# Attention of a prefix-GQA trunk layer: exponentials left in PSUM for 38 of 64 latent heads, turned before they are normalised, and a new order of the stage

## The chip, the core and the metric

The kernel runs on one core of one Trainium2 chip. The metric is the device time of one execution in microseconds. TensorE is PE, VectorE is DVE, ScalarE is ACT, GpSimd is POOL, SyncE is SP; PEld is TensorE's loading of the stationary operand, and SPq is SP's sequencer, which issues the DMAs.

## What is computed

One trunk layer for 128 context tokens and 512 latent tokens, in float32 (the products are made of a rounded high part and a low part, three matmuls for one). What the change touches is the attention of the mixer; 16 query heads share 4 key and value heads of 64 columns.

```python
def one_block(qblk):
    s = jnp.einsum('bqkgd,btkd->bkgqt', qblk, k).astype(jnp.float32) * scale
    p = jax.nn.softmax(s, axis=-1).astype(v.dtype)
    return jnp.einsum('bkgqt,btkd->bqkgd', p, v)
...
    u = rms_norm(h, p["g_pre1"]) * (1 + sc1) + sh1
    mo, k, v = mixer(u, p, rope_tabs, ctx_k, ctx_v)     # q, k normed and rotated, then block_attention, then w_att_out
    h = h + g1 * rms_norm(mo, p["g_post1"])
    u = rms_norm(h, p["g_pre2"]) * (1 + sc2) + sh2
    h = h + g2 * rms_norm(conv_ffn(u, p), p["g_post2"])
```

Context tokens attend to the 128 context keys, latent tokens to 128 cached keys and 512 latent keys, 640 in all.

## The kernel before

**Stages.** A first stage (0 to about 66 us) makes the modulated tokens `UH`, `UL` (high and low part) and the products for keys and values. The attention stage (66 to 268 us) is what the change is about. Behind it come the output projections, the convolution mixer and the feed-forward layer, which are long runs of matmuls against weights that stream in.

**The attention stage is a list of pieces and a plan.** The code makes `works`: each `Work` has a name, an engine (sometimes two or three to choose from), the works it comes after, and `Room`s, places in memory that it shares with other works. The string `PLAN` then gives the order in which the pieces are written out: a number of a work, a letter for the engine chosen, and digits for the places taken (`follow`, L705). On PE, ACT, DVE, POOL and SP the instructions stay in this order; each engine runs its own in order, and waits where its next one is not ready. So a piece that is late holds up whatever stands behind it on its engine.

**One step.** 36 steps: four groups of heads, each with one step for the context tokens (steps 0, 9, 18 and 27, four heads of 128x128 at once) and eight for latent tokens (128 query rows, two heads, written n.0 and n.1). A latent step goes so:

- `s` (L1107, PE): scores of both heads, 12 matmuls into two areas of PSUM, 640 columns each. There are three areas of two banks each (`AREAS`); two more banks, 6 and 7, hold query tiles, gate products and outputs.
- `max` (L1152, DVE): the negated row maximum, read from PSUM.
- `exp` (L1155, ACT): the exponential, from PSUM into one of four tiles `E` of SBUF; its row sum is accumulated. With it the area of PSUM is free.
- `part` (L1075, POOL or DVE) and `inv` (L1077, DVE): the sum times 2 to the power -15, and its reciprocal, one pair for each head.
- `share` (L1167, POOL), for the 25 heads that `POOL_WAY` marks: E times the reciprocal.
- `P1` (L1170, ACT): the high half of the probabilities as float16, for the other 39 heads with the reciprocal as a scale.
- `P2` (L1175 POOL for the 25, L1177 DVE for the 39): the low half, E (times the reciprocal) minus P1. P1 and P2 lie in one of four tiles `P`.
- `T` (L1185, SP): a DMA that transposes the tile `P` into one of five tiles `PT`.
- `pv` (L1204, PE): 30 matmuls of `PT` with the values, into bank 6 or 7. After two steps the output is complete: `AH` (L1214, ACT) writes its high part, scaled by the values' factor, `AL` (L1217, DVE) the low part, and the bank is free.

**Around it** in the same lists: the query tiles (`q` matmuls L693; `rot` L831 and L832, `add` L852, `sum` L856, `factor` L859 on POOL, `norm` L874; `turn` L1057, `hi` L1059 on ACT, `lo` L1061 on DVE), the cutting of weights (`hi` L808 on ACT, `lo` L813 in two halves on DVE or POOL), the gate products, and `ada` matmuls with 128 moving columns in float32 (L292), four of them side by side in the array.

**The end of the stage.** PE's list ends with the last `pv`, some gate matmuls (L693), and goes on to the first output projection (L237 to L239), which reads AH and AL.

Of the kernel before, what the change touches and what calls it, by code (L numbers as in the profile page):

```python
# [12 lines left out]
F32 = mybir.dt.float32  # L13
# [3 lines left out]
ALU = mybir.AluOpType  # L17
# [31 lines left out]
68a0 41a 1a0 121a 31a 12a10 122a 24a0 123a 21a 69a 42a21 13a 14a1 67a 0a 22a32 11a 43a 70a 2a2 6a 15a 23a 3a 34a1 71a 25a 44a2  # L49
4a 35a 51a0 80a1 73a0 26a 5c0 81a 16a 45a 52a2 27c1 7a 32a01 82a 46a 74a 8a4 17c2 33b 83a 53a 75a 72a0 28a3 84a12 9a 93a2 47c3  # L50
36a 10a 54a0 94a 76b 85a 55a 77a4 95a 86a1 37b4 58a0 60b1 78a0 29a 38a0 59b2 139a 96a 30a 56a1 65a 97a20 140b 18a3 63a 57a 66a
108a1 61a 64b 98b 39a 62a 109a 19a 40a 141b 99a2 110a 20a 48a2 100a 144a 79a 111a 101a 49a 87a 367a1 50a 114a0 88a 126a0 102b
368a 103a4 89a 115a 127a 369a3 112a01 116a 90a2 128a 113b 91a1 117a 106a1 370b 104a2 371a 92a 372a 105a 379a10 107a 373a3 129a
145a 380a 374a 118a4 382a 132a2 142a1 119a3 146b 375a1 381a1 147a 143a 120a 383a2 384a 133a 396a12 385a 186a 130a22 134a 388a1
386b 148a 131b 389a 135a 124a2 397a 390a0 399a 376a0 398a0 149a 125a 184a 387a 377a 401a 185a 391a 400a3 402a 414a01 378a 150a1
405a2 158a0 403a 415a 392a0 136a4 406a 151a1 159a 393a 416a1 404a 417a 407a4 160a 137a0 408a3 419a 138a 420a 161a 152a 418a0
423a 394a2 409a 431a02 164a0 162a00 421a 424a1 153a 410a3 171a1 422a 434a 215a 187a3 154a 432a 435a2 425a 217a 155a0 433a3 261a
172a 188a 260a 438b 163b 156a1 439a 450a21 165a 436a 426a1 427a2 443a 437a 157a 216a 440a0 411a0 451a 220a 166a 444a3 395a 428a
452a1 167a 173a 453a 429a3 412a 445a 413a 454a0 168a2 174a 455b 441a 169a2 467a21 457a 446a4 177a2 456a 458a 170a 459a 463a1
175a21 189a0 468a 442a0 176a 470a 190a 469a2 464a 430a1 460a2 472a 473a 471a3 178a 465a2 461a 486a02 476a3 474b 475a 191a 487a  # L60
179a 462a1 447a 477a 488a0 479a 180b 478a3 192a 491b 448a 489a 480a0 502a10 449a 193a12 490a1 481a 202a1 492a 503a 495a1 181a4
505a 504a2 203a 493a 482a0 194a 496a 182a3 204a 507a 506a3 508a 183a 497a4 511a 521a1 494a 195a1 509b 498a2 510a 466a0 196a 522a
515a3 197a 499a 533a20 523a0 198a 516a 500a1 205a 534a 512a0 524a 199a3 483a 206a00 517a2 200a0 513a 535a1 525a 201a 536a 484a
550a12 208a0 538a 514a0 485a 537a3 526a 539a 209a 218a1 553a 542a1 540a 210a 501a0 541a 551a 527a2 554a2 528b 545a 219a 221a
543a 529a3 569a02 557a 207b 552a0 223b 558a 211b 518a 544a1 222a 546a3 555a 572a 291a 562a 224a 556a 262a 570a 519a 212a3 225a
547a 292a 563a0 520a 213a1 571a1 226a2 234a0 214a 564a 548a4 293a 559a2 586a10 574b 227a2 575a 560a 573a3 578a 565a0 530a1 587a
235a 531a 576a 579a1 532a 561a2 236a 577a 589a 588a2 580a 228a 237a 590a0 296a 591b 592a 604a21 229a 595a3 238a11 581a3 593b
582a0 239b 549a1 230a 594a 596a 240a1 566a 598a2 583a 597a1 231a2 605a 567a 247a0 232a2 568a 584a4 606a1 233a 248a 599a 609a
620a02 610a 607a 600a0 613a1 249a 241a 608a2 623a 242a 263a1 611b 621a 624a3 243a 614a 250a 622a0 337a 627a 336a 264a 244a3 628a
615a2 625a 253a0 612a 639a20 626a 633a3 251a02 629a 245a3 585a1 254a 616a0 640a 255a 630a2 601a 617a 641a1 631a 265a0 642a 618a3  # L70
602a 644b 246a 643a2 266a 645a 603a 252a 632a4 634a 656a21 256a 646a 267a 648a 647a 635a0 657a 652a1 675a0 659a 658a0 268a 653a
649a0 661a 257a1 662a 660a3 676a 654a1 650a 269a20 258a0 687a21 677a2 259a 665a 663b 270b 278a1 664a 688a 669a2 678a 690a 279a
271a2 666a3 272a 636a0 679a 670a 273a 689a1 619a 680b 691a3 671a0 692a 667a 693a 274b 705a02 637a 694b 695a 681a1 638a 651a4
280a 297a 696a 682b 708a 275a3 281a 668a2 276a1 700a 706a 709a0 294a0 299a 707a2 683a3 712a 298a 295a 701a2 710a 713a 282a11
724a20 717a 697a0 338a 711a 277a 284a1 283b 300a 984a 725a 702a 655a1 727a 718a3 698a 285a 726a3 672a 985a 703a1 714a1 986a
741a12 286a 729b 673a 730a 715a 987a 728a1 301a 699a4 719a 674a 742a 310a1 303a0 716a0 744a 743a2 731a 339a2 287a 732a 302a0
733a2 736a 304a 684a0 720a2 340a 745a0 746b 734a 761a10 305a 737a0 747a 748b 991a 311a 749a 764a 995a 685a 738a 735a3 288a4 762a
765a3 312a 306b 289a2 750a 313a 768b 686a 763a1 769a 290a 307a2 316a2 323a0 773a 766b 751a1 767a 314a22 778a21 770a3 317a 754a
315b 774a2 704a1 771a 308a3 781a 721a 775a 739a1 309a 782a1 324a 779a 752a 722a 772a4 785b 796a01 786a 780a3 723a 325a 783a 797a
776a0 318a 1019a1 799a 798a2 326a 319a 753a2 784a 740a1 755a0 327a10 801a 756a 802a 328b 814a20 790a3 329a1 791a 341a0 805a  # L80
800a0 757a1 815a 787a2 342a 817a 803a 792a3 816a1 833a1 788a 343a 806a1 819a 834a 818a3 807a 320a4 820a 804a 344a 330a 321a0
821b 823a0 758a 822a 322a 345a01 331a 835a2 845a02 824a 789a1 809a 332b 759a 836b 333a3 848a 347a0 825a2 826a 810a3 354a0 760a
849a1 348a 777a1 846a 349a 334a1 852b 837a 355a 853a 838b 808a0 811a 827a2 335a 793a 346b 988a 350b 861a21 828a 812a4 839a0 990a
847a0 840b 356a 989b 829a1 794a 864a 351a2 357a 352a2 795a 850a 865a3 353a 841a3 996a1 851a 358a22 854a1 868a 880a01 869a 862a
359a 857a3 873a 997a 855a 863a2 883a 360a2 998a 866a 874a2 867a 881a 813a0 884a0 875a 858a 870a0 830a 856a0 887b 361a 882a1 888a
871a 896a21 362a 831a 859a4 992a 999a 832a 363a 897a 885a 364a2 994b 1000a 1001a0 876a1 886a 899a 365a3 898a3 842a1 366a 993b
1002a 889a1 872a2 901b 902a 843a 915a02 905a 890a 900a2 844a 1003a 891a3 892a3 903a 918a 860a1 906a2 904a 893a 919a1 907a 916a
1004a 894a0 909a0 922b 931a12 923a 1005a 910a 917a0 908a4 877a 932a 927a1 920a 921a 1006a0 934a 933a3 911a1 928a 1007a 878a 936a
935a2 950a01 879a 929a2 937a 924a3 938a 895a1 939a 951a 943a 940a2 925a 1008a 952a1 941a 926a0 912a 944a0 955a 956a 953a 945a
966a20 913a 942a3 954a0 914a 1009a 967a 959a1 957a 946a1 1011a1 969a 1010a 968a3 960a 930a1 970a2 971a 972a 958a 961a4 975a3  # L90
1012a 973a 974a 978a2 976a 1013a 1020a 979a 977a0 947a 962a0 980a2 1014a 948a 963a 949a 1015a 964a1 1016a 1017a 981a0 965a 1018a
# [2290 lines left out]
```

## Time and profile before

| | |
|---|---|
| three runs | 1118.48, 1118.0, 1113.09 us; median 1118.0 |
| the profiled execution | 1114.35 us, span of its instructions 1112.6 us |
| busy, share of the span | PE 96%, PEld 89%, DVE 80%, ACT 53%, POOL 15% |
| mean granted TensorE clock | 0.992 of full speed |

The shares are means over stages with different limits. Behind the attention stage PE is never idle for long; inside it no engine is full all the time, and the question is which one the others wait for. The rows of the stage are shown in the prediction. A group's row reads: line, engine, operation, output and inputs by name, shapes, count | busy time in us, mean ns of one | idle time ahead of it and what ended it. A row of one line's instructions reads: count, shortest/median/longest in ns, first and last start in us.

### The profile page before, as it was taken

To read this page: it belongs to the slowest core of one execution; us is meant where nothing else is said; L and a number is where in the kernel's file an instruction comes from. 1 tells how busy PE (TensorE), PEld (TensorE's weight loads), DVE (VectorE), ACT (ScalarE), POOL (GpSimd) and SP (SyncE) were. 2 spreads that over 40 slices of the span, in tenths; PEclk is the share of its full clock that TensorE was granted. 3 is DMA by queue.
4 is the path that set the end of the run, shared out by engine and by line. 5 is a ranking of instruction groups with operands and counts; after the bars stand their busy time and mean duration, and the time that the engine had idled before them with its cause. 6 is when DMAs were issued, how large, how long until landed. Compare 5 with 4: busy or idle time off the path is not lost.

```text
span 1112.6 us, 20087 instructions
## 1 busy us (share of the span) xinstructions
PE 1072.7 (96%) x7973; PEld 994.5 (89%) x7973; DVE 884.7 (80%) x1341; ACT 584.3 (53%) x1043; POOL 164.7 (15%) x204
## 2 busy tenths in 40 slices
PE   8989898789999999999999999999999999999997
PEld 5777787678999999999999789999999999998886
DVE  5699999886549899988578558898899889989544
ACT  5467777675334445445522256655555555546442
POOL 1068868761000000000000021000000000000001
PEclk9999989899999999999999999999999999999999
DMA  9838998795224423332264654233344333435722
GB/s 316 235 111 177 159 196 170 131 186 109 75 78 129 125 78 91 105 99 78 77 189 152 211 170 151 77 100 119 119 126 138 101 117 117 129 100 184 260 93 94
DMA packets 245611, 152.15 MB, mean 137 GB/s; under 512 B 94602, under 2 KB 224134, under 8 KB 245518
## 3 DMA queue, kind: packets, MB, share of 16 engines
q1 hardware_dynamic: 245406, 150.84, 49.8%
q8 instruction: 62, 1.02, 0.4%
q14 instruction: 31, 0.25, 0.1%
q10 hardware_dynamic: 112, 0.04, 0.0%
HBM read 117.39 MB, written 11.44 MB: 116 GB/s over the span
## 4 chain that ended last, share of the span: by engine, by line
PE 80%; DVE 9%; DMA 4%; ACT 2%; issue 2%; POOL 2%; SPq 0%; DVEq 0%; ACTq 0%; POOLq 0%
PE b L1302 46%; PE b L237 10%; PE b L239 9%; PE b L238 9%; DVE marks L1152 2%; DMA PT<-P 2%; DVE P L1177 2%; PE s L693 1%; DVE wlo L813 1%; DMA raw<-in_w_in_dram 1%; DMA araw<-in_w_ada_dram 1%; PE s L1107 1%; PE b L1901 1%; ACT E L1155 1%; DVE QF L852 1%
## 5 line engine op out<-in xcount | busy, mean ns | idle before, releaser
L1302 PE MATMUL b<-ZBr,whi 128*128 128x320 f32 x688 | 152.1, 309 | 0.0
L1302 PE MATMUL b<-MT,whi 128*128 128x320 f32 x608 | 134.2, 309 | 0.0
L1302 PEld LDWEIGHTS b<-ZBr,whi 128*128 128x128 f32 x688 | 115.0, 188 | 0.1
L1302 PE MATMUL b<-ZBr,wlo 128*128 128x320 f32 x344 | 106.1, 309 | 0.0
L1302 PEld LDWEIGHTS b<-MT,whi 128*128 128x128 f32 x608 | 101.6, 188 | 0.0
L1302 PE MATMUL b<-MT,wlo 128*128 128x320 f32 x304 | 94.0, 309 | 0.0
L1289 ACT ACTIVATE whi<-SUM 128x1024 fp32r<-128x1024 f32 x40 | 42.2, 1055 | 78.8 <-DVE SUM L1816 76.3
L1846 DVE SCALAR_TENSOR_TENSOR Y<-C,cffn,Y 128x642 f32<-128x642 f32 x88 | 77.5, 881 | 0.9
L203 DVE TENSOR_TENSOR wlo<-raw,whi 128x1024 fp32r<-128x1024 f32 (+1 forms) x31 | 34.2, 1102 | 53.7 <-ACT whi L202 53.5
L1302 PE MATMUL b<-ZBT,whi 128*128 128x320 f32 x320 | 71.1, 309 | 0.0
L1302 PE MATMUL b<-UL,whi 128*128 128x320 f32 x228 | 70.8, 311 | 0.0
L1302 PE MATMUL b<-UH,wlo 128*128 128x320 f32 x228 | 70.1, 307 | 0.0
L1302 PE MATMUL b<-UH,whi 128*128 128x320 f32 x228 | 69.7, 306 | 0.0
L1289 ACT ACTIVATE whi<-WB 128x1024 fp32r<-128x1024 f32 x38 | 40.1, 1055 | 55.4 <-DVE WB L1397 55.4
L1293 DVE TENSOR_TENSOR wlo<-raw,whi 128x1024 fp32r<-128x1024 f32 (+1 forms) x51 | 50.4, 1018 | 21.5 <-ACT whi L1289 21.5
L1302 PEld LDWEIGHTS b<-ZBr,wlo 128*128 128x128 f32 x344 | 64.6, 188 | 0.0
L1310 ACT ACTIVATE p<-b 128x320 f32<-128x320 f32 x78 | 34.1, 438 | 55.5 <-PE b L1302 53.7
L2244 POOL TENSOR_TENSOR ssqs<-ssqs 128x1 f32<-128x1 f32 x4 | 0.8, 194 | 417.2 <-ACT JK L2237 417.2
L1714 POOL TENSOR_SCALAR ssq<-ssq 128x1 f32<-128x1 f32 x5 | 1.4, 289 | 391.0 <-DMA raw<-in_w_up_dram 389.5
L1155 ACT ACTIVATE E<-s,marks 128x640 f32<-128x640 f32 x64 | 50.5, 791 | 14.6 <-DVE marks L1152 12.6
L1302 PEld LDWEIGHTS b<-MT,wlo 128*128 128x128 f32 x304 | 57.1, 188 | 0.0
L1302 PEld LDWEIGHTS b<-ZBT,whi 128*128 128x128 f32 x320 | 54.3, 188 | 1.7
(419 smaller groups left out, 3360.7 us busy)
## 6 DMA issues: line engine op xcount, KB each, us to landing
raw<-in_w_in_dram SPq DMA_DIRECT2D x48, 512.0 KB
RAW<-in_w_up_dram SPq DMA_DIRECT2D x40, 512.0 KB
raw<-in_w_down_dram SPq DMA_DIRECT2D x22, 512.0 KB
raw<-in_w_ada_dram SPq DMA_DIRECT2D x16, 512.0 KB
actd<-Y SPq DMA_DIRECT2D x18, 321.0 KB
XT<-in_w_ada_dram SPq DMA_DIRECT2D x9, 512.0 KB
raw<-in_w_att_out_dram SPq DMA_DIRECT2D x8, 512.0 KB
raw<-in_w_conv_out_dram SPq DMA_DIRECT2D x8, 512.0 KB
```

The lines of the kernel that those rows point to most:

```text
L203: V.tensor_tensor(out=lo[:, :n], in0=raw, in1=hi[:, :n].bitcast(F32), op=ALU.subtract)
L237: PE.matmul(out, ah, bh, start=start, stop=False)
L238: PE.matmul(out, ah, bl, start=False, stop=False)
L239: PE.matmul(out, al, bh, start=False, stop=stop)
L1152: lambda s_of=s_of, mk=mk, h=h: V.tensor_reduce(out=mk[:, h:h + 1], in_=s_of(), axis=AX.X, op=ALU.max, negate=True),
L1155: lambda s_of=s_of, er=er, mk=mk, h=h: S.activation(slot(ES, er), s_of(), AF.Exp, bias=mk[:, h:h + 1], accum_out=mk[:, 4 + h:5 + h]), [mx] ...
L1177: V.scalar_tensor_tensor(out=p2, in0=slot(ES, er), scalar=r, in1=p1, op0=ALU.mult, op1=ALU.subtract)
L1289: S.activation(to[0], raw, AF.Copy)
L1293: V.tensor_tensor(out=lo, in0=raw, in1=hi.bitcast(F32), op=ALU.subtract)
L1302: PE.matmul(out, p[:, ws], q[:, k, :], start=start and k == 0 and n == 0, stop=stop and k == 3 and n == 2, skip_group_check=True)
L1310: S.activation(t, pair[j][b], AF.Copy)
L1846: V.scalar_tensor_tensor(out=y, in0=crows(j)[i][:, d:d + NACT], scalar=cffn[:, 44 * d + o:44 * d + o + 1], in1=y, op0=ALU.mult, op1=ALU.add)
```

## The change

- For the first head of every latent step and for the second head of six of them (38 of 64) the exponential is written back into the area of PSUM that the score lies in. P1 (ACT) and P2 (DVE) read it there, and the area is free only after P2. For the other 26 (the second head of a step, as the new `POOL_WAY` marks) it goes to a tile `E` of SBUF, and P2 is made on POOL.
- Nothing is multiplied by a reciprocal before the transposing DMA: `part` and `share` are gone. P1 and P2 are the two halves of the exponential times 2 to the power 15: a constant scale in the first heads, a constant that is added to the maximum (one more small DVE instruction) in the second heads and the context steps.
- One reciprocal for both sums of a step. `pv` begins with matmuls that spread the reciprocal sums over 64 partitions (the column of `marks` broadcast as stationary operand, the identity as moving operand, 128 columns in float32): 80 of them in all, into the upper half of the bank that takes the output.
- Once the output is complete, four pieces follow instead of two: `R` (ACT) copies the spread reciprocals to SBUF, `O` (DVE) multiplies the output in place by them and by the values' factor, then `AH` (ACT) and `AL` (DVE).
- Two tiles `E` instead of four, five `P` instead of four, six `PT` instead of five.
- A new `PLAN` and `POOL_WAY`. By it all 18 halves of weight cutting that lay on DVE (11) or POOL (7) in this stage are on POOL; of 16 `add` 11 and of 20 `norm` seven go from DVE to POOL; three scalings of values and their low parts move one each from DVE to POOL; eight small normings of keys leave ACT, two pieces for POOL.

```diff
-POOL_WAY = "0100100110010010010110000010101011010111010011010001001000010000"
+POOL_WAY = "11111110100111111011101111111110"
...
-        NE, NP_, NT_, NZ, NX, NF, NQ = 4, 4, 5, 3, 3, 3, 4
+        NE, NP_, NT_, NZ, NX, NF, NQ = 2, 5, 6, 3, 3, 3, 4
...
+                    way = pool_way(n, h)
+                    held_in = er if way else ar[h]
+                    def e_of(er=er, s_of=s_of, way=way):
+                        return slot(ES, er) if way else s_of()
+                    def most(s_of=s_of, mk=mk, h=h):
+                        V.tensor_reduce(out=mk[:, h:h + 1], in_=s_of(), axis=AX.X, op=ALU.max, negate=True)
+                        if h:
+                            V.tensor_scalar(out=mk[:, 1:2], in0=mk[:, 1:2], scalar1=SHIFT * math.log(2), scalar2=None, op0=ALU.add)
...
-                    def share(er=er, r=r):
-                        G.tensor_tensor(out=slot(ES, er), in0=slot(ES, er), in1=r.broadcast_to((128, NTOK)), op=ALU.mult)
-                    def first(er=er, pr=pr, r=1.0 if way else r):
-                        S.activation(slot(PS, pr)[:, 0:NTOK], slot(ES, er), AF.Copy, scale=r)
+                    def first(e_of=e_of, pr=pr, h=h):
+                        S.activation(slot(PS, pr)[:, 0:NTOK], e_of(), AF.Copy, scale=1.0 if h else 2.0 ** SHIFT)
-                        if way:
-                            G.tensor_tensor(out=p2, in0=slot(ES, er), in1=p1, op=ALU.subtract)
+                        if h:
+                            (G if way else V).tensor_tensor(out=p2, in0=e_of(), in1=p1, op=ALU.subtract)
                         else:
-                            V.scalar_tensor_tensor(out=p2, in0=slot(ES, er), scalar=r, in1=p1, op0=ALU.mult, op1=ALU.subtract)
+                            V.scalar_tensor_tensor(out=p2, in0=e_of(), scalar=2.0 ** SHIFT, in1=p1, op0=ALU.mult, op1=ALU.subtract)
+                    h1 = work(f"P1 {n}.{h}", "ACT", first, [ex], [held_in, pr])
+                    h2 = work(f"P2 {n}.{h}", "POOL" if way else "DVE", second, [h1], [held_in, pr])
...
+                        PE.matmul(p[64 * h:64 * h + 64, 256 + 128 * i:384 + 128 * i], mk[:, c:c + 1].broadcast_to((128, 64)), ident,
+                                  start=True, stop=True, tile_position=(0, 64 * h), skip_group_check=True)
...
+                def spread(pvr=pvr, xr=xr):
+                    S.activation(slot(XS, xr), at_bank(pvr)[:, 256:512], AF.Copy)
+                def whole(pvr=pvr, u=u, xr=xr):
+                    p = at_bank(pvr, 256)
+                    V.scalar_tensor_tensor(out=p, in0=p, scalar=u, in1=slot(XS, xr), op0=ALU.mult, op1=ALU.mult)
```

**What moves on DVE.** Steps 13 and 14, before the change: from the maximum of 13.1 on, `part`, `inv`, the query tile's `rot` and `add`, the two P2 of 13.0 and 12.1 (they read `E`), and the maximum of 14.0. Areas of PSUM are `s_99`, `s_100`, `s_101` here and below; `s_94` and `s_98` are the banks 6 and 7.

```order
L1152 TENSOR_REDUCE marks<-s_99_837 128x1
L856 TENSOR_REDUCE ssqs<-Z_732 128x4
L1075 TENSOR_SCALAR marks<-marks 128x1
L1077 RECIPROCAL marks<-marks 128x1
L831 TENSOR_TENSOR X_734<-s_94_756,tabq 128x256
L832 TENSOR_TENSOR QF_737<-s_94_756,tabq 128x256
L1075 TENSOR_SCALAR marks<-marks 128x1
L852 TENSOR_TENSOR QF_737<-QF_737,X_734 128x256
L1077 RECIPROCAL marks<-marks 128x1
L1177 SCALAR_TENSOR_TENSOR P_724<-E_719,marks,P_724 128x640
L1177 SCALAR_TENSOR_TENSOR P_721<-E_720,marks,P_721 128x640
L1152 TENSOR_REDUCE marks<-s_100_855 128x1
```

After the change, from P2 of 13.0 over the maxima of step 14 and P2 of 14.0 to the maxima of step 15:

```order
L1162 SCALAR_TENSOR_TENSOR P_723<-s_100_867,P_723 128x640
L1144 TENSOR_REDUCE marks<-s_99_847 128x1
L1059 TENSOR_TENSOR QT_742<-s_94_756,QT_742 128x256
L1144 TENSOR_REDUCE marks<-s_101_874 128x1
L1146 TENSOR_SCALAR marks<-marks 128x1
L853 TENSOR_REDUCE ssqs<-Z_732 128x4
L828 TENSOR_TENSOR X_733<-s_98_816,tabq 128x256
L829 TENSOR_TENSOR QF_736<-s_98_816,tabq 128x256
L1168 RECIPROCAL marks<-marks 128x2
L1162 SCALAR_TENSOR_TENSOR P_721<-s_99_847,P_721 128x640
L1144 TENSOR_REDUCE marks<-s_100_867 128x1
L1144 TENSOR_REDUCE marks<-s_101_874 128x1
```

Between two P2 of first heads there stand now the next step's maxima; P2 reads an area of PSUM, and `add`, `part` and one of the reciprocals are not on this engine any more.

**What moves on ACT.** Before, step 13: both exponentials into `E`, P1 of 13.0, 12.1 and 13.1 (`P<-E`), AH of an earlier step and two pieces of query tiles (`Z`, `QT`), then the exponential of 14.0.

```order
L1155 ACTIVATE E_719,marks<-s_101_876,marks 128x640
L1155 ACTIVATE E_717,marks<-s_99_837,marks 128x640
L1170 ACTIVATE P_724<-E_719,marks 128x640
L1170 ACTIVATE P_721<-E_720,marks 128x640
L854 ACTIVATE Z_731<-s_94_756 128x4x64
L1170 ACTIVATE P_723<-E_717,marks 128x640
L1214 ACTIVATE AHa<-s_98_816,vcol 128x2x128
L1059 ACTIVATE QT_741<-s_99_837 128x256
L1155 ACTIVATE E_718,marks<-s_100_855,marks 128x640
```

After, from the exponentials of step 13 (13.1 into `E`, then 13.0 in place) to those of step 14 (14.0 in place, then 14.1):

```order
L1149 ACTIVATE E_717,marks<-s_101_874,marks 128x640
L1149 ACTIVATE s_100_867,marks<-s_100_867,marks 128x640
L1210 ACTIVATE AHa<-s_94_756 128x2x128
L1155 ACTIVATE P_723<-s_100_867 128x640
L1155 ACTIVATE P_719<-E_717 128x640
L1057 ACTIVATE QT_742<-s_94_756 128x256
L1149 ACTIVATE s_99_847,marks<-s_99_847,marks 128x640
L851 ACTIVATE Z_732<-s_98_816 128x4x64
L1149 ACTIVATE E_718,marks<-s_101_874,marks 128x640
```

P1 of a head now follows its exponential on the same engine, with nothing of another engine between them.

191 lines of the change are left out of this document (87 added, 104 removed).

## The prediction

> **What bounds the kernel now.** I read the windows by stage first (stretch, its length, busy time of each engine with instructions, granted clock, share of the DMA engines, GB/s):
>
> ```profile
> 66.00:88.00 22.00, 20.16 (x192) 18.61 (x193) 19.96 (x43) 13.22 (x36) 16.22 (x16) 0.92 0.12 35
> 88.00:262.00 174.00, 150.46 (x1987) 130.47 (x1986) 156.71 (x316) 129.53 (x282) 124.13 (x128) 0.96 0.92 173
> 262.00:268.00 6.00, 4.46 (x74) 3.57 (x73) 0.48 (x1) 0.80 (x2) 0.00 (x0) 1.00 0.56 115
> 268.00:600.00 332.00, 332.00 (x2272) 330.95 (x2271) 260.34 (x350) 145.59 (x220) 0.00 (x0) 1.00 0.35 104
> 600.00:1112.00 512.00, 506.82 (x2999) 466.12 (x2997) 405.03 (x530) 258.23 (x429) 13.93 (x36) 1.00 0.42 134
> ```
>
> From 268 us on PE is full (332.0 of 332, 506.8 of 512): what the attention stage gains or loses passes on whole. In the stage DVE is fullest, 156.7 of 174 (90%; PE 86%, ACT 74%, POOL 71%), and its 17 us of idle time are waits. The steps run from the first transposing DMA to the last:
>
> ```profile
> L1142 SPq DMA_TRANSPOSE PT<-P x4: 1232/1292/1386, 87.9 to 226.8; - x4
> L1185 SPq DMA_TRANSPOSE PT<-P x64: 1307/1474/3990, 92.4 to 262.1; - x64
> ```
>
> So 35 steps in 262.1 - 87.9 = 174.2 us, 4.98 each. The groups of 64 to 270 us give prices:
>
> ```profile
> L1152 DVE TENSOR_REDUCE marks<-s 128x1 f32<-128x640 f32 x64 | 50.8, 810 | 2.5 <-PE s L1107 2.5
> L1155 ACT ACTIVATE E<-s,marks 128x640 f32<-128x640 f32 x64 | 50.5, 791 | 14.6 <-DVE marks L1152 12.6 <-POOL marks L1075 0.6 <-DVE marks L1077 0.6
> L1177 DVE SCALAR_TENSOR_TENSOR P<-E,marks,P 128x640 f16<-128x640 f32 x39 | 39.5, 1022 | 3.6 <-ACT P L1170 3.4
> L1170 ACT ACTIVATE P<-E,marks 128x640 f16<-128x640 f32 x39 | 31.7, 825 | 9.6 <-DMA PT<-P 6.4 <-DVE marks L1077 1.6 <-ACT E L1126 0.7
> L1170 ACT ACTIVATE P<-E 128x640 f16<-128x640 f32 x25 | 18.2, 732 | 8.4 <-DMA PT<-P 5.9 <-POOL E L1167 2.5
> L1077 DVE RECIPROCAL marks<-marks 128x1 f32<-128x1 f32 x64 | 9.7, 156 | 5.1 <-POOL marks L1075 4.1
> L1075 DVE TENSOR_SCALAR marks<-marks 128x1 f32<-128x1 f32 x24 | 3.4, 142 | 0.9 <-ACT E L1155 0.9
> L1138 DVE TENSOR_TENSOR P<-E,P 128x512 f16<-128x512 f32 x3 | 3.5, 1166 | 0.0
> L813 DVE TENSOR_TENSOR wlo<-raw,whi 128x512 fp32r<-128x512 f32 x11 | 13.6, 1253 | 0.0
> L852 DVE TENSOR_TENSOR QF<-QF,X 128x256 f32<-128x256 f32 x11 | 9.2, 833 | 0.0
> L874 DVE TENSOR_TENSOR QF<-QF,rq 128x256 f32<-128x256 f32 x8 | 8.8, 1097 | 0.1
> L1217 DVE SCALAR_TENSOR_TENSOR AL<-s,vcol,AHb 128x256 fp32r<-128x256 f32 x10 | 4.7, 474 | 6.0 <-ACT AHb L1214 6.0
> L1061 DVE TENSOR_TENSOR QT<-s,QT 128x256 fp32r<-128x256 f32 x20 | 8.1, 411 | 3.5 <-ACT QT L1059 3.5
> L912 DVE TENSOR_TENSOR KL<-s,KH 128x512 fp32r<-128x512 f32 x4 | 2.6, 674 | 0.0
> L1135 ACT ACTIVATE P<-E 128x512 f16<-128x512 f32 x4 | 2.5, 626 | 1.2 <-POOL E L1132 1.2
> L869 ACT ACTIVATE PT<-P,rk 128x128 f32<-128x128 f32 x15 | 4.6, 388 | 0.0
> L1271 ACT ACTIVATE MA<-s 128x640 f32<-128x640 f32 x1 | 0.7, 688 | 0.0
> L1059 ACT ACTIVATE QT<-s 128x256 fp32r<-128x256 f32 x20 | 7.5, 380 | 3.6 <-PE s L1057 3.5
> L1214 ACT ACTIVATE AHb<-s,vcol 128x256 fp32r<-128x256 f32 x10 | 4.7, 469 | 6.1 <-PE s L1204 6.1
> L1175 POOL TENSOR_TENSOR P<-E,P 128x640 f16<-128x640 f32 x25 | 38.0, 1525 | 11.6 <-ACT P L1170 11.4
> L1167 POOL TENSOR_TENSOR E<-E,marks 128x640 f32<-128x640 f32 x25 | 34.3, 1378 | 4.8 <-DVE marks L1077 4.6
> L1075 POOL TENSOR_SCALAR marks<-marks 128x1 f32<-128x1 f32 x40 | 14.2, 355 | 20.8 <-ACT E L1155 20.6
> L813 POOL TENSOR_TENSOR wlo<-raw,whi 128x512 fp32r<-128x512 f32 x7 | 10.3, 1473 | 0.6 <-ACT whi L808 0.6
> ```
>
> Behind each exponential the sum crosses from ACT to POOL or DVE (L1075), to DVE (L1077), for 25 heads to POOL (L1167), and back to ACT. POOL waits 20.6 us at L1075, ACT 12.3 us before P1 for a free tile P (`DMA PT<-P`).
>
> **The work that changes, DVE.** P2: 39 of 1.022 us go, 38 from PSUM come. A P2 from PSUM isn't in the trace; bounds are 0.81 (L1152 reads the same 640 columns there) and 1.02 (L1177's mean). Why L1177 is slow shows in the spread:
>
> ```profile
> L1177 DVE SCALAR_TENSOR_TENSOR P<-E,marks,P x39: 846/882/1789, 91.5 to 260.1; 128x640 f16<-128x640 f32 x39
> L813 DVE TENSOR_TENSOR wlo<-raw,whi x11: 674/1471/1773, 88.1 to 224.4; 128x512 fp32r<-128x512 f32 x11
> L1217 DVE SCALAR_TENSOR_TENSOR AL<-s,vcol,AHb x10: 465/470/484, 193.4 to 267.1; 128x256 fp32r<-128x256 f32 x10
> ```
>
> The two with both inputs in SBUF are now short, now twice as long; the one that reads PSUM never varies (465 to 484 ns) though POOL works beside it as often. P2 from PSUM has one input in SBUF, so I take L1177 undisturbed, 0.87, between its shortest and its median. The Trainium skill (SBUF — State Buffer, Who interferes with whom) says that a DVE instruction with two SBUF inputs contends with GpSimd reads and one with a single SBUF input does not; by that rule the 38 cost the 33.1 us taken here, by the row's mean they would cost 38.8 and the sum below be 6 us less.
>
> - P2: -39.5 + 38 x 0.87 = -6.4
> - reciprocals, 64 to 32: -9.7 + 5.0 = -4.7
> - weight cutting -13.6, `add` -9.2, seven `norm` of 1.097 -7.7, all to POOL: -30.5
> - AL without a scale, 20 at 0.41 (L1061) for 0.473: -1.2; context P2, four at 0.674 (L912, the same 512 columns from PSUM) for three of 1.166: -0.8; four scalings and low parts of 512 columns at about 0.8: -3.3
> - added: 20 `O` at 0.474, as L1217 with its scale (as it writes PSUM too, 0.47 to 0.6) +9.4; eight constants at 0.142 +1.1
>
> Sum -36 us of the 177 that DVE is busy from 66 to 268 us (-31 with P2 at 1.02, -39 at 0.81).
>
> **ACT.** P1 becomes 38 x 0.69 (L1271, PSUM to SBUF) + 26 x 0.73 + four of 0.58 (L1135 less the same 0.04) = 47.5 for 31.7 + 18.2 + 2.5; 20 `R` at 0.38 (L1059, the same 256 columns) +7.6; AH at 0.38 for 0.469 -1.8; eight normings of keys at 0.388 -3.1: -2 in all. No row shows ACT writing PSUM; I take 0.79 as into SBUF. Bounds of 0.69 (L1271) and 0.88 (0.1 each way) would move 38 heads by 3.8 us.
>
> **POOL** loses 34.3 + 14.2, and some 5 of context steps and others, and gets 11 cuts at 1.47, 18 pieces of query tiles at about 0.8 and a few more P2 and key pieces: by some 15 us it ends lighter, near 110. Its P2 then comes straight behind P1. **PE** gets 80 spreading matmuls, in pairs side by side:
>
> ```profile
> L292 PE MATMUL s<-raw,s 128*32 128x128 f32 x128 | 4.3, 275 | 0.5 <-DMA raw<-in_w_ada_dram 0.5
> ```
>
> Four of the same 128 float32 columns take 4.3 / 32 = 0.134 us, so 40 pairs 5.4 us. I cost them at nothing: PE's 23.5 idle us of the stage cover them; uncovered they are the 5.4.
>
> **The path.** With DVE at 141 and ACT at 128 no engine is full any longer, and latency decides: an area is now held until P2. So I walk the new lists: from P2 of one first head over DVE's rows to the next step's first maximum, over ACT's rows from its exponential to P1, and to P2. Step 14 (rows shown with the change): maximum 0.81, exponential 0.79, `Z` 0.38, second exponential 0.79, P1 0.69, two hand-overs 0.1, P2 0.87: 4.4 us. Step 13 has a query tile's sum and rotation (3 x 0.41) and the constant (0.14) ahead of the first exponential, and AH in the place of `Z`: 5.8. Of 35 steps 21 are such full loops, 115.9 us together at these prices (mean 5.5, from 4.4 to 7.9 where a context step or two outputs lie on the way). In the 14 others the step's first maximum stands ahead of the P2 before it, their exponentials run while that loop is still open, and only DVE's rows from P2 to P2 are added, 29.7 us (2.1 each). Walk: 146 us for 174.2 now. It leaves out waits for PE, POOL and DMA; today DVE's idle time is 17 us, with those for ACT, which the walk holds already, among it. I take two thirds, 11: 157, 4.5 a step, -17.2.
>
> The end of the stage:
>
> ```profile
> 262.10 3.42 DMA PT<-P
> 265.56 1.00 PE s L1204 x29
> 266.56 1.07 PE s L693 x6
> ```
>
> Behind the last `pv` AH and AL (0.94) are covered by six gate matmuls (1.07). Now R, O, AH, AL make 0.38 + 0.47 + 0.38 + 0.41 = 1.64, with hand-overs 1.9, and twelve gate matmuls (2.14) stand there. The six more used to fill a wait ahead of the last `pv`, which stays: +1.1.
>
> Sum: -17.2 + 1.1 = -16.1 on the profiled 1114.35 (span 1112.6 and 1.7 around it): 1098. The median of the runs is 3.65 higher: **1102 us**, own range 1094 to 1110 (P2 and ACT's writes at either bound, waits of 5 to 20 us).
>
> **Rivals.**
>
> *The waits vanish (B).* An instruction right behind another starts about 0.1 us before that one ends, which the walk doesn't count (0.2 a step, 7 us). With 7 us of waits the steps take 146: -28.2 + 1.1, 1091. For it: exponential to P1 is now one engine's affair. Against it: the list of PE puts query and gate pieces between scores.
>
> *The transposes set the pace (C).* DMA engines are 92% busy from 88 to 262 us, 160 us of 174, and none of that goes. If their packets can't be packed tighter than 0.95, the steps take 169: -5.2 + 1.1, 1114. For it: ACT's 12.3 us of waits for a tile P. Against: a fifth P and a sixth PT are there, and the share isn't a capacity, as it passes 1 in short stretches:
>
> ```profile
> 110.00:120.00 10.00, 7.87 (x109) 6.74 (x109) 8.64 (x18) 5.91 (x15) 7.17 (x8) 1.00 1.20 209
> ```
>
> *PSUM is held too long (D), slower.* With three areas, a score needs two while the third holds a first head up to P2. Where the score comes late, DVE stands at the maximum with the open P2 behind it, and short steps become full loops of 5.5 for 2.1. From five of the 14 on the gain of 17.2 is eaten (5 x 3.4); I price it at nine: 157 + 31 = 188, +13.8 + 1.1, 1133. For it: the walk's full loops are already longer than today's 4.98. Against: ACT has no hand-over ahead of P1. The Trainium skill speaks for D (PSUM — Partial Sum Buffer, Summary: rules for kernel authors): evacuate promptly, PSUM is tight. No row here shows it, as today an area is free after the exponential.
>
> *The order doesn't do what it says:* if E, two tiles, held ACT until POOL's P2 (1.5 us in a queue with cuts of 1.47), this would look like C.
>
> **Chances.** Forecast 0.45, B 0.17, C 0.20, D 0.18. A change under 0.5% (5.6 us) is about what can't be told from none. Faster: 0.43 + 0.17 + 0.08 of C = 0.68; same: 0.16 (most of C's rest); slower: 0.16. The range takes in B and C with some 3 and 7 us beside them, 1088 to 1121, and leaves out most of D and a part of B.
>
> **What would show it.** Right: the last transpose starts near 245 us, DVE's busy time in the stage near 141 with P2 near 0.85 and nothing over 1, POOL off ACT's waits. Wrong: last transpose at 258 or later; scores waiting for P2, or maxima for scores, in total over 20 us (D); ACT waiting for `DMA PT<-P` or for POOL over 15 us (C); an exponential into PSUM over 0.9 or a P2 over 1.0.

## The result, and the profile after

The changed kernel takes 1105.7 us (median of 5 runs, 1103.0 to 1107.0), the kernel before 1117.9 (5 runs beside them, 1113.1 to 1118.5): ratio 0.990, 95% interval 0.987 to 0.993. It is faster by 1%, and the time lies in the range given.

The two profiled executions, both at a mean granted clock of 0.992, differ by 7.4 us of span (1112.6 and 1105.2). Their medians differ by more. The profiled execution of the changed kernel was the slowest of its five runs, and the kernel before mostly ran at a lower clock than its profiled execution: of its 62 runs on the four chips of the experiments, 50 had less than 0.992. On one chip its runs at 0.982 to 0.984 took 1119 to 1120 us, those at 0.993 to 0.995 1113 to 1115.

The windows by stage of the changed kernel (stretch, length, busy time of PE, PEld, DVE, ACT and POOL, granted clock, DMA share, GB/s), cut at its first and last transpose:

```profile
66.00:80.00 14.00, 12.35 (x160) 10.71 (x159) 13.75 (x30) 8.52 (x23) 13.17 (x14) 1.00 0.15 44
80.00:252.00 172.00, 156.56 (x2102) 137.25 (x2104) 133.03 (x289) 132.50 (x304) 96.18 (x93) 0.97 0.98 175
252.00:260.00 8.00, 8.00 (x130) 7.34 (x126) 1.67 (x4) 1.84 (x5) 0.00 (x0) 1.00 0.62 83
```

And its rows of the transposes (count, shortest/median/longest ns, first and last start):

```profile
L1166 SPq DMA_TRANSPOSE PT<-P x64: 1291/1437/4522, 85.7 to 252.2; - x64
L1127 SPq DMA_TRANSPOSE PT<-P x4: 1232/1243/1369, 79.9 to 216.3; - x4
```

VectorE is relieved as forecast in kind: 133 busy of 172 us, where it was 157 of 174. GpSimd is at 13.2 + 96.2 = 109 us, forecast near 110. Yet the steps are hardly shorter: first transpose to last is 252.2 - 79.9 = 172.3 us, before it was 174.2. What did move is the first transpose, from 87.9 to 79.9.

So the kernel can be cut at three events that every trace shows: the first transpose, the last one, and the first matmul of the output projection (L237 before, L233 after). From that matmul to the end it is 844.9 us in both. The differences of the first three pieces then add up to the whole:

| us, profiled executions | before | after | difference |
|---|---|---|---|
| first transpose starts | 87.94 | 79.88 | -8.06 |
| first to last transpose (35 steps) | 174.16 | 172.33 | -1.83 |
| last transpose to first output projection | 5.55 | 8.11 | +2.56 |
| from there to the end | 844.9 | 844.9 | 0 |

**What the steps wait for.** The chain of waits is followed back from the end, at each step to what ended the wait. By line, its shares of 66 to 268 us are these, first before the change, then after it (the view ends the rows where they end here):

```profile
by line: DVE marks L1152 12.8%; DMA PT<-P 11.4%; issue 9.3%; DVE P L1177 8.8%; PE s L693 7.2%; DVE wlo L813 5.0%; PE s L1107 3.6%; ACT E L1155 3.4%; DVE QF L852 3.2%; DVE QF L874 2.7%; POOL rq L859 2.3%; DVE marks L1077 2.1%; DVE ssqs L856 
by line: PE s L689 17.3%; DMA PT<-P 16.8%; PE s L1097 9.5%; PE s L1191 7.1%; issue 6.0%; ACT s L1149 4.7%; ACT P L1155 4.3%; DVE marks L1144 3.4%; DVE P L1162 2.6%; POOL wlo L810 2.5%; PE s L1183 2.1%; ACT E L1149 1.9%; POOL P L1160 1.7%; A
```

VectorE's lines led the chain before; after, TensorE's and the transposes do. The chain alone doesn't say which of the two is the limit; the experiments have to. In the changed kernel (start, length, what), these are the transposes on it; the pieces left out between them are engines' work:

```profile
96.65 5.84 DMA PT<-P
...
106.92 5.96 DMA PT<-P
...
139.51 4.75 DMA PT<-P
...
178.51 7.01 DMA PT<-P
...
199.28 5.02 DMA PT<-P
...
238.54 5.28 DMA PT<-P
```

34 us of the chain are transposes on their way, 5 to 7 us each. The issuing instruction takes 1.4 us in the median; the rest is the transfer and what it waits for. The list of waits (who waits for whom: us, times, longest) shows little of it: while a transpose is on its way TensorE works through gate and query matmuls, and only what is left over counts as waiting:

```profile
PE s L1191 <- DMA PT<-P: 9.7, 5, 3.2
POOL P L1160 <- DMA PT<-P: 5.1, 1, 5.1
ACT P L1155 <- DMA PT<-P: 3.8, 4, 1.8
```

**The prices.** The groups of the changed kernel, to be read beside those of the prediction (maxima and first halves are left out where they did not change):

```profile
L1162 DVE SCALAR_TENSOR_TENSOR P<-s,P 128x640 f16<-128x640 f32 x32 | 26.3, 822 | 5.2 <-ACT P L1155 4.7
L1160 DVE TENSOR_TENSOR P<-s,P 128x640 f16<-128x640 f32 x6 | 4.9, 823 | 1.0 <-ACT P L1155 1.0
L1160 POOL TENSOR_TENSOR P<-E,P 128x640 f16<-128x640 f32 x26 | 36.6, 1408 | 35.6 <-ACT P L1155 30.5 <-DMA PT<-P 5.1
L810 POOL TENSOR_TENSOR wlo<-raw,whi 128x512 fp32r<-128x512 f32 x18 | 22.8, 1286 | 2.6 <-ACT whi L805 2.5
L1149 ACT ACTIVATE s<-s,marks 128x640 f32<-128x640 f32 x38 | 29.3, 771 | 13.4 <-DVE marks L1144 8.6 <-DVE marks L1146 3.9 <-PE s L1055 0.6
L1155 ACT ACTIVATE P<-s 128x640 f16<-128x640 f32 x38 | 27.0, 713 | 0.7 <-DMA PT<-P 0.4
L1183 PE MATMUL s<-ident,marks 128*64 128x128 f32 x160 | 16.4, 292 | 1.6 <-ACT gate L1236 1.0 <-DVE AL L1213 0.4 <-DVE QF L829 0.2
```

P2 (0.82 us for 0.87) and the exponentials into PSUM (0.77 for 0.79) came out under the price taken, P1 from PSUM a little over it (0.71 for 0.69). The spreading matmuls (L1183) did not come near theirs: 160 records of 16.4 us, where the prediction had 5.4. Each of the 80 is two records.

**Why the steps start earlier.** The chains of waits ahead of the first transpose. Before, VectorE scales the values (E<-VV), halves them (VV) and adds up a query tile (QF) ahead of its last pieces for keys and queries, behind which the first score stands:

```profile
72.20 1.79 DVE E L967
...
76.35 0.68 DVE VV L976
77.03 1.43 DVE QF L852
78.45 0.60 DVE VV L976
79.06 1.20 DVE KL L912 x2
```

After, the first score (L1097) and its maximum (L1109) come first, and the values (P<-VV at L965) behind them:

```profile
73.43 0.83 PE s L1097 x12
74.29 0.70 DVE marks L1109
75.01 0.17 DVE marks L1110
75.18 0.59 DVE P L965
...
79.19 0.66 DVE P L1125
```

Not all of the 8.06 us is the new order. In the profiled execution of the kernel before, TensorE's granted clock was 0.5 for 3.4 us from 67.3 us on, ahead of the first score, which makes the 0.92 of the row from 66 to 88 us in the prediction. Two experiments below (e5 and e6) run the kernel before with nothing altered up to its first transpose. Both had a clock of 1.00 there, and it started at 85.2 and 85.5 us. The row of e5:

```profile
66.00:88.00 22.00, 19.66 (x197) 17.64 (x196) 20.71 (x42) 14.15 (x37) 17.60 (x17) 1.00 0.16 34
```

A second profile of the changed kernel (e11) started at 79.2. So by these executions some 6 us belong to the order, and the other 2 come with the clock of one execution.

### The profile page after: what moved, and what is told of

The parts are those of the page before. It is cut to its first block, busy times and chain, and to the rows that moved or that the text cites. A ratio compares the mean times of both kernels' runs of the same rounds, so it can differ in the third digit from the quotient of the medians.

```text
span 1105.2 us, 20360 instructions
## 1 busy us (share of the span) xinstructions
PE 1078.5 (98%) x8133; PEld 1001.8 (91%) x8133; DVE 856.6 (78%) x1307; ACT 584.1 (53%) x1055; POOL 135.3 (12%) x168
## 4 chain that ended last, share of the span: by engine, by line
PE 87%; DMA 4%; DVE 3%; ACT 3%; issue 1%; POOL 1%; SPq 0%; DVEq 0%; ACTq 0%; POOLq 0%
PE b L1300 46%; PE b L233 10%; PE b L235 10%; PE b L234 10%; PE s L689 3%; DMA PT<-P 3%; PE s L1097 2%; PE s L1191 1%; PE s L233 1%; ACT s L1149 1%; PE s L235 1%; ACT P L1155 1%; PE s L234 1%; PE s L464 1%; DMA XT<-in_x_sample_dram 1%
## 5 line engine op out<-in xcount | busy, mean ns | idle before, releaser
L199 DVE TENSOR_TENSOR wlo<-raw,whi 128x1024 fp32r<-128x1024 f32 (+1 forms) x31 | 34.2, 1102 | 50.2 <-ACT whi L198 49.9
L1144 DVE TENSOR_REDUCE marks<-s 128x1 f32<-128x640 f32 x64 | 51.4, 816 | 4.7 <-PE s L1097 4.7
L1291 DVE TENSOR_TENSOR wlo<-WB,whi 128x1024 fp32r<-128x1024 f32 x38 | 46.5, 1223 | 8.7 <-ACT whi L1287 8.6
L1287 ACT ACTIVATE whi<-raw 128x1024 fp32r<-128x1024 f32 (+1 forms) x51 | 43.5, 892 | 17.6 <-PE b L235 10.4
```

Of the source, the lines that this page charges most:

```text
L199: V.tensor_tensor(out=lo[:, :n], in0=raw, in1=hi[:, :n].bitcast(F32), op=ALU.subtract)
L1144: V.tensor_reduce(out=mk[:, h:h + 1], in_=s_of(), axis=AX.X, op=ALU.max, negate=True)
L1287: S.activation(to[0], raw, AF.Copy)
L1291: V.tensor_tensor(out=lo, in0=raw, in1=hi.bitcast(F32), op=ALU.subtract)
```

## The experiments

The theories that stood against each other: TensorE has become the bound (P); the transposes pace the steps (T), by the sum of their packets (T1) or by the latency of single ones (T2); VectorE does (D, in the kernel before V). The table has the profiled execution of each kernel cut as above, worked out from the starts in its trace; from the first output projection on all of them take 844.9 to 845.2 us. "Ratio" is to the kernel before on the same chip; the experiments ran on several chips, and differences of 1 or 2 us between medians of different chips say nothing by themselves.

| kernel | first T | steps | tail | median us | ratio (95%) |
|---|---|---|---|---|---|
| before | 87.9 | 174.2 | 5.5 | 1117.9 | |
| changed | 79.9 | 172.3 | 8.1 | 1105.7 | 0.990 (0.987 to 0.993) |
| e1 spread twice | 78.8 | 172.4 | 7.1 | 1103.6 | 0.988 (0.985 to 0.990) |
| e2 spread in one pass | 80.4 | 170.2 | 6.6 | 1103.9 | 0.988 (0.985 to 0.990) |
| e3 cuts back on VectorE | 80.6 | 176.1 | 7.6 | 1113.9 | 0.997 (0.995 to 0.998) |
| e4 half transposes | 77.1 | 163.1 | 7.9 | 1095.0 | 0.980 (0.978 to 0.983) |
| e5 before, half transposes | 85.2 | 167.1 | 5.6 | 1104.2 | 0.989 (0.986 to 0.991) |
| e6 before, cuts on GpSimd | 85.5 | 181.0 | 5.6 | 1118.2 | 1.001 (0.9995 to 1.003) |
| e7 late first score | 83.2 | 172.3 | 8.2 | 1109.7 | 0.994 (0.991 to 0.996) |
| e8 more packets | 79.4 | 178.9 | 7.8 | 1114.4 | 0.998 (0.997 to 1.000) |
| e9 three loads behind | 79.0 | 168.1 | 8.2 | 1103.6 | 0.989 (0.987 to 0.991) |
| e10 values first | 83.0 | 173.9 | 7.4 | 1110.7 | 0.995 (0.993 to 0.997) |
| e11 changed, again | 79.2 | 172.4 | 7.5 | 1104.8 | 0.990 (0.987 to 0.992) |
| e12 three loads, again | 79.3 | 169.5 | 7.4 | 1103.2 | 0.989 (0.986 to 0.991) |

**e1: the spreading matmuls twice.** My first theory behind the result was P: by the windows above TensorE has only 194 - 176.9 = 17 us without a matmul from 66 to 260 us, and the spreading had cost three times its price.

```diff
-                for i in range(2) if t == 0 else (pi,):
+                for i in 2 * ((0, 1) if t == 0 else (pi,)):
```

> Every spreading matmul is issued twice (the second writes the same numbers). In the changed kernel TensorE stands idle for only 17.1 us between 66 and 260.3 us, and the spreading matmuls take 13.5 us of it. Theory P (TensorE has become the bound of the stage): the second set adds 13.5 us of work and the kernel gets 10 to 14 us slower than the changed kernel, near 1117. Theory T (the transposing DMAs pace the steps, TensorE waits for them): the work goes into the idle time, +0 to +3. Theory D (VectorE and its hand-overs pace the steps, as the prediction had it): likewise +0 to +3.

Measured: 1103.6 us, not slower at all, the steps 172.4. The group and the window of the steps show that the work was there, 320 records, and that TensorE took it into its holes:

```profile
L1183 PE MATMUL s<-ident,marks 128*64 128x128 f32 x320 | 25.5, 286 | 0.7 <-DVE AL L1213 0.5 <-DVE QF L829 0.2
...
79.00:251.00 172.00, 164.57 (x2290) 145.60 (x2292) 133.72 (x290) 133.45 (x306) 96.05 (x93) 0.98 0.99 175
```

TensorE is busy 164.6 of 172 us instead of 156.6, in steps of the same length. The second set added 8 us there, not the 13.5 expected, but by P even those would have shown. P falls.

**e2: the spreading in one pass.**

```diff
+        rh = at.tile([128, 8, 4], mybir.dt.bfloat16, name="rh")
+        identh = at.tile([128, 128], mybir.dt.bfloat16, name="identh")
...
-V.reciprocal(mk[:, 8:10], mk[:, 4:6])
+V.reciprocal(mh[:, 0:2], mk[:, 4:6])
...
-PE.matmul(..., mk[:, c:c + 1].broadcast_to((128, 64)), ident, ...)
+PE.matmul(..., mh[:, c:c + 1].broadcast_to((128, 64)), identh, ...)
```

> The reciprocal sums are written as bfloat16 (rounded to 8 bits) and spread by bfloat16 matmuls with a bfloat16 identity, one pass in the place of two slow ones: the 13.5 us should fall to 2 to 4. P: the kernel gets 6 to 11 us faster than the changed one, 1095 to 1100. T and D: only the three spreadings behind the last transpose are on the path, -1 to -2.

Measured: 1103.9 us, 1.8 under the changed kernel. That is what T and D gave it, not P. But e1, with twice the spreading, has the same median, so it is not shown that the 1.8 come from the spreading. The spreading matmuls took 9.0 us instead of 16.4, not the 2 to 4 expected, so P was tested less hard here than its range supposed.

**e3: the cuts back on VectorE.** The letters of 20 pieces in the plan (18 weight cuts, and two low halves of the values):

```diff
-140b 141b ... 147b 146b ... 905b
+140a 141a ... 147a 146a ... 905a
```

> The 20 weight cuts (low halves) that the change put on GpSimd go back to VectorE at the same places of the order: VectorE gets 14 to 25 us more to do (0.7 to 1.25 us each), near 165 us of the stage. P: VectorE has room, -1 to +4. D: VectorE was what paced the stage and relief of it brought the gain, +8 to +20, back to the kernel before or behind it. T: -1 to +4.

Measured: 1113.9 us, +8.2, the foot of what D gave and twice the most that T and P gave; by the profiles +4.0, but the profiled execution is the fastest of the twelve, at a clock of 0.998, where the others had 0.989 to 0.994. VectorE was busy 159.8 us from 66 to 264 us, 11 more than in the changed kernel. Its load still counts: with these pieces on VectorE two thirds of the gain are gone. This is more than undoing the change, though: of the 20 pieces, seven cuts and one low half of the values were on GpSimd before it too.

**e4: half transposes.**

```diff
-nc.sync.dma_start_transpose(slot(PT, tr), slot(PS, pr))
+nc.sync.dma_start_transpose(slot(PT, tr)[:, 0:5, :], slot(PS, pr)[:, 0:NTOK])
...
-slot(PT, trs[h])[:, 5 * part + k, :]
+slot(PT, trs[h])[:, k, :]
```

> The transposing DMAs carry only the first half of each tile P (the high parts), and the pv matmuls read that half for both: the low parts are left out of the result, the number of matmuls and everything else stay. TensorE's three long waits (3.2, 2.6 and 2.4 us) each end with such a DMA. P: transposes are late only there, -2 to -6. T: the DMA engines, with a share of 1.0 through the stage, pace the steps, and half of the bytes bring -10 to -20. D: -1 to -3.

Measured: 1095.0 us, -10.7, steps of 163.1. The window of its steps, 77 to 240 us:

```profile
77.00:240.00 163.00, 154.46 (x2149) 135.45 (x2142) 134.22 (x293) 132.98 (x307) 98.21 (x95) 1.00 0.63 119
```

The share of the DMA engines falls from 0.98 to 0.63, no engine's work changes, and TensorE is busy 154 of 163 us. The steps are 9.2 us shorter: the transposes hold them up in the changed kernel, as T has it. (The first one also started 2.8 us earlier, which the edit doesn't explain.) That TensorE would be the next limit is likely from this row, and wasn't tried.

**e5: the same in the kernel before.** The same edit at L1142, L1185 and L1203.

> The kernel before, with the same cut of the transposing DMAs to the high parts as in the run before (the low parts are left out of the result). There it was worth 10.7 us on the changed kernel. Theory V (before the change VectorE paced the steps, as the prediction had it, and the transposes came to the front only with its relief): 0 to -4 against the kernel before. Theory T (the transposes, 159 us of packets in 174, paced the steps already): -7 to -12.

Measured: 1104.2 us, -12.2 against the kernel before on this chip, all that T gave. But the edit's own share is smaller: the steps are 7.0 us shorter than in the profile of the kernel before, 2.8 are the earlier start with the faster clock, and the rest is the difference between profile and median. The window of its steps:

```profile
85.00:252.00 167.00, 149.73 (x1983) 129.64 (x1982) 156.20 (x315) 130.86 (x284) 125.92 (x129) 0.96 0.57 116
```

VectorE's 156 us, the bound in the prediction, fit into 167 once the transposes are halved. So the transposes held up the steps of the kernel before as well, by 7 us, and VectorE stood closely behind them.

**e6: VectorE's cuts on GpSimd, in the kernel before.** The letters of 11 pieces:

```diff
-147a 217a 216a 222a 292a 293a 299a 298a 985a 986a 990a
+147b 217b 216b 222b 292b 293b 299b 298b 985b 986b 990b
```

> The kernel before, with the 11 weight cuts of VectorE (13.6 us) sent to GpSimd at the same places of the order: this part of the change alone. V: -3 to -8 against the kernel before, unless GpSimd, with 124 + 16 us of 174, holds the second halves of P up. T: 0 to -2, or slower by GpSimd's queue.

Measured: 1118.2 us, no change. In the profile the first transpose came 2.5 us earlier, ahead of every piece that was moved, and the steps took 181.0. The wait that grew, from 4.1 us in the kernel before, is the reciprocal's for the constant that GpSimd makes:

```profile
DVE marks L1077 <- POOL marks L1075: 11.8, 14, 1.9
```

In this kernel the sum of most heads crosses GpSimd, and behind cuts of 1.5 us it comes late. So moving the cuts alone is worth nothing. That it pays once the sums are off GpSimd is argued from this wait; a relief of VectorE that loads no other engine was not tried in the kernel before.

**e7: a late first score.** Four pieces of a query tile go ahead of the first score (367a2) in the plan:

```diff
+108a2 109a 110a 111a 367a2
-367a2 ... 108a2 ... 109a ... 110a ... 111a
```

> The changed kernel with the four pieces of q03 (24 matmuls, 3.6 us) put ahead of the first score in TensorE's order: the steps start some 3.6 us later and TensorE has that much less to do among them. If the steps run at a pace of their own (transposes or VectorE), the late start goes through: +2.5 to +4, near 1109, with the last transpose as much later. If the end is set by the sum of TensorE's work, or if slack takes it up: 0 to +1.

Measured: 1109.7 us, +4.1; first transpose +3.3, steps the same 172.3, though TensorE had 24 matmuls less to do in them. A late start is not made up. (From 66 to 88 us the granted clock was 0.92, where the changed kernel had 1.00, so the 3.3 may hold some of that.)

**e8: more packets.**

```diff
+        spare = at.tile([128, 8, 16], F32, name="spare")
...
+                nc.sync.dma_start(spare, units[10][0][0:1024, 0:16].rearrange("(k p) c -> p k c", p=128))
```

> The changed kernel; behind each of the 19 weight loads of the stage's order one more load goes out, 64 KB in 1024 packets of 64 bytes, into a tile that nothing reads. At 12 to 26 ns a packet (the 256 byte ones take 26) this is 0.8 to 1.7 us on the 16 DMA engines each, 13 to 28 us in the steps. Theory T1 (the engines are full, 167 us of packets in 172, and their sum sets the pace): +10 to +25. Theory T2 (only the latency of single transposes counts, those that TensorE waits for): +1 to +6.

Measured: 1114.4 us, +8.7; steps 178.9, +6.6. The packets were cheaper than I had put them, and fewer fell into the steps: 14 of the 19 loads, 14,336 packets at 11 ns, 9.8 us on 16 engines. Neither range holds: T1's +10 stood on dearer packets, T2 gave at most +6. For what the packets did cost, two thirds are in the steps and nearly all in the median, which is T1 in kind.

**e9: three loads less in the steps.** Load 906a goes behind the last transpose:

```diff
-902a 655a0 674a 906a 308a3
+902a 655a0 674a 308a3
...
-847a 925a 883a3 861a2
+847a 925a 883a3 906a 861a2
```

> The changed kernel with the load of weight unit 19 taken from its place behind unit 18 (186.7 us) to behind the last transpose; the two loads that follow it in the queue (220.7 and 230.4 us) go there with it, all of them for the stage that follows. Twelve such loads took 23.2 us of packets, so three take 5.8. Theory T1 (the sum of the packets sets the pace): the last transpose starts 4 to 6 us earlier and the kernel gets 3 to 6 us faster than the changed one, 1100 to 1103. Theory T2 (latency of single transposes): -0.5 to -2. If the following stage then waits for its weights, this is given back: 0 to +6.

Measured: 1103.6 us, 2.0 under the changed kernel's 1105.7, with 4.2 us less in the steps of the profile. Since the two disagreed, both were run again on one chip.

> The changed kernel itself, unaltered, on the same chip as the next run, since the median with the three loads moved (1103.6 us) lies only 2.0 us under that of the changed kernel on another chip (1105.7) while its profiled span was 4.9 us shorter. 1103 to 1107 is expected by every theory.

> The three loads behind the last transpose, repeated beside the changed kernel on one chip. Theory T1 (the sum of the packets sets the pace, three loads are 5.8 us of them): 3 to 5.5 us below the run beside it. Theory T2 (latency of single transposes): 0 to 2 below it.

Measured: 1104.8 and 1103.2, 1.6 us apart, steps 172.4 and 169.5. The two ratios' intervals overlap (0.987 to 0.992 and 0.986 to 0.991), so it is not shown that this version beats the changed kernel. Both times the median misses T1, which gave 3 to 6, and lies in the range of T2. The steps of the profiles get shorter by 3.0 to 4.2 us for 5.8 of packets taken away: the sum of the packets counts in part.

**e10: the values first.** Ten pieces of the values go between the first score (367a2) and its maximum (368a), on the engines that they had before the change; two small ones that they need go ahead of the score:

```diff
+55a 56a3 367a2 58a4 60b1 59b0 65a 63a 57a 66a 61a 64b 62a ... 368a
-367a2 55a ... 368a ... 58b4 56a3 ... 57a 60a1 ... 59a0 ... 66b ... 64b ... 62a
```

> The changed kernel with one part of the new order undone: the scaling and halving of the values (five operations on VectorE, as before the change) stands ahead of the first maximum again, nothing else moves. If this is what let the steps start earlier, the first transpose comes 4 to 7 us later and the kernel gets 4 to 7 us slower, 1110 to 1112. If the start is set by the queries' and keys' chain, or the steps catch up: 0 to +2.

Measured: 1110.7 us, +5.1; first transpose +3.2, less than the 4 to 7 expected, steps +1.6. Its row of the context transposes and, ahead of it in the chain of waits, the scaling that is back on VectorE:

```profile
73.21 2.34 DVE P L926 x2
...
L1088 SPq DMA_TRANSPOSE PT<-P x4: 1235/1243/1368, 83.0 to 222.5; - x4
```

So this part of the new order is worth some 3 us of the early start, and some 2 more behind it. The four query pieces of e7 are another: before the change they stood ahead of the first score too, and there they are worth 3.3. Together that is about the 6 us put down to the order above, but the two were not undone together, and here too the clock from 66 to 88 us was lower (0.85) than in the changed kernel.

## Why the prediction was right, and where not

The direction and the range held: 1102 forecast, 1105.7 measured. The sum behind it did not, and that the time lies so near the forecast is in good part luck. For the profiled execution the sum had -16.1, and -7.4 came; by medians it was -12.3, because the kernel before was mostly run at a lower clock than in its profile and the profiled execution of the changed kernel was its slowest. Of the table's first three rows none has the size that the prediction gave it: the gain forecast for the steps hardly came, and an earlier start, which had no term, stands in its place.

**The steps: 157 forecast, 172.3 measured.** The step that failed is "no engine is full any longer, and latency decides", with the walk over VectorE's and ScalarE's rows that came of it. The walk held the transfers only as part of 11 us of waits. The rows shown had the DMA engines at 92% of 174 us, 160 us, and none of that was to go. The prediction put the case aside with "the share isn't a capacity, as it passes 1 in short stretches". Ten microseconds at 1.20 say nothing of what can be kept up over 170; e4, e5 and e8 show how little was left: with the transposed bytes halved the steps lost 9.2 and 7.0 us, with 9.8 us of packets more they grew by 6.6. Rival C had the steps at 169, nearer than any other case, at a chance of 0.20.

**VectorE as the bound.** This was read from 90% busy with 17 us of waits. e5 took nothing from VectorE and shortened the steps by 7.0 us; the change relieved VectorE and shortened them by 1.8. VectorE was the second limit, close behind; e3 shows that it is felt again as soon as its load is raised.

**The start: no term in the sum.** The steps were counted from 87.9 us, as if that were given. It is the largest term, -8.06, some 6 of it by the order, and e7 and e10 show that such a shift reaches the end: +3.3 became +4.1, +3.2 became +5.1. The new order of the front was there to be read in the plan: the first score stands four pieces of TensorE's list earlier.

**The tail: +1.1 forecast, +2.56 measured.** The step that failed is that the wait for the last transpose "stays". Before, the chain held 3.42 us of it, and TensorE was busy 4.46 of the 6 us from 262 to 268. After, nothing waits for it: TensorE is busy 8.00 of the 8 us from 252 to 260, and from 246 us to the first output projection the chain runs through TensorE alone, which still has older work when the last transpose starts at 252.2:

```profile
252.07 0.84 PE s L1191 x30
252.91 1.08 PE s L689 x6
253.98 0.37 PE s L1183 x4
254.35 0.84 PE s L1191 x30
255.19 1.94 PE s L689 x12
257.13 0.37 PE s L1183 x4
257.50 0.84 PE s L1191 x30
258.33 1.97 PE s L689 x12
```

These are gate matmuls of 5.0 us in all, three `pv` and two spreadings of 0.37. In e2 a spreading there takes 0.18, which is 0.4 us for the two. Its tail is shorter by 1.5, but the unaltered kernel's was 8.1 and 7.5 in two executions, and 7.1 with the spreading doubled (e1).

**The spreading: 5.4 if uncovered, taken as nothing.** The price was a third of the 16.4 us measured: L292's four records share 0.134 us, four records of L1183 (one pair of matmuls, two records each) take 0.37 in the chain. Costing it at nothing in the steps was right all the same, as e1 showed with twice the work.

**The rest.** P2 from PSUM took 0.822 us where 0.87 was forecast, and it was never stretched (809 to 826 ns); by this the trace agrees with the rule of the Trainium skill that was weighed (SBUF — State Buffer, Who interferes with whom: outside its 2-port modes, a VectorE instruction with a single SBUF input does not contend with GpSimd), and the row's mean of 1.02 would have been wrong. Exponentials into PSUM took 0.771, against 0.797 into SBUF and 0.79 forecast. VectorE's busy time fell by 29 us (177.2 from 66 to 268 us; 148.5 from 66 to 260), forecast 36. The forecast added up lengths of instructions, and these did fall by 37; but neighbours on the engine overlap, by 23 us in all before and 14 after, so the busy time fell by less.

**The rivals.** D asked for over 20 us of scores waiting for P2 or maxima for scores; the trace has 4.7 for maxima and 0.8 for scores that wait for P2, the loading of their weights included. B, the waits gone and the steps at 146, did not come. C's own sign, ScalarE waiting over 15 us for a tile P, was not there (3.8) although its mechanism was: the wait sat in TensorE, and only the chain and the experiments showed it.

**Open.** Why the steps follow the packets only in part (two thirds of 9.8 added, half to three quarters of 5.8 taken away, a ninth to a seventh of the 64 and 66 that halving takes away) isn't settled. The packets' own time is elastic: the 256 byte packets of the transposes took 25 ns on average in the kernel before, 26 after, with a median of 18 in both, so the sum of 167 us in 172 holds waiting as well. Whether the number of packets or their bytes costs the time was not tried. Nor was SP's own queue, a rival to the packets: issuing the 68 transposes keeps it 118 us of the 172 (94 in e4), and the 14 loads of e8 add 7 us to that, so the experiments change both together. And the transposes are not the only limit: e3 asks 11 us more of VectorE, leaves the transposes alone, and costs 8.2.

## What to carry to other kernels

Cut both traces at events that exist in each (first and last transfer of the loop, first matmul behind it) and forecast every piece, the start among them. A walk over steps forecasts one piece.

A resource that is over 90% busy for a whole stage is a candidate for the bound, DMA engines too, even where no list of waits has much of it. Halve its work, in the kernel before as well, and see; doubling a suspected cost is the quickest way to clear it.

## What the runs showed of the hardware

Transposing DMAs were slow: 83,652 packets of 256 bytes, 21.4 MB, took 136 us of 16 engines, 157 GB/s by the packets' own times and whatever waiting they hold, while the weight loads in 512 byte packets took 30 ns each, some 270 GB/s. The Trainium skill (DMA: Bandwidth & Descriptors, Latency and other measured facts) has 261 GB/s for one kernel's transposes with a non-contiguous middle dimension and 350 to 400 for contiguous ones. As an estimate from its 261, the transposes here would have taken 82 us of the 172; the trace doesn't agree, and the measurement decides.

With VectorE's P2 reading PSUM, the operations with two inputs in SBUF got faster on the engine beside it: GpSimd's P2 went from 1525 to 1408 ns on average (1394 to 1422), its weight cuts from 1473 to 1286. And in e3 VectorE's 18 cuts took 785 ns, where the 11 of the kernel before took 1253. That the P2 are the cause was not set apart: other operations with two inputs in SBUF left VectorE too.

Across these runs the granted clock went with TensorE's holes: e1, with 7 us of them in its steps, ran at 0.995 to 0.998, the kernel before, with 24, at 0.982 to 0.995.
